# A decoder trunk on one core: where layer A's last block lies, when layer B's query weights are loaded, and which queue copies the window cache

## The chip, the cores and the metric

The kernel runs on one core of a Trainium2 chip. The metric is the device time of one execution in microseconds (us); lower is better.

## The reference

Four layers, A B C A, run over 1024 prompt tokens and 32 sample tokens (8 sequences of 4 new tokens, each with a cache of 4096 old ones), with width 1024. Every layer is `x = LayerNorm(ALPHA*x + mixer(x))`.

```python
def short_conv_mixer(x, buf, w_in, conv_w, w_out):            # layers 0 and 3 ("A")
    h, b_gate, c_gate, z = jnp.split(x @ w_in, 4, axis=-1)
    conv, new_buf = causal_dwconv(c_gate * h, buf, conv_w)
    return (jax.nn.silu(z) * b_gate * conv) @ w_out, new_buf
```

Layer 1 ("B") is an attention with three branches: keys and values compressed by blocks of 32 tokens, 16 selected blocks of 64 tokens, and a window of 512 tokens. The sample sequences read old keys and values through a page table, out of a paged cache (`cache_nsa_kv`) and a window cache (`cache_nsa_win`). Layer 2 ("C") is a gated linear recurrence. Besides the trunk's output the caches are returned. One of these outputs, `nsa_win_sample`, is the window cache moved on by four rows: 508 old rows of each of the 8 sequences, copied, and 4 new rows behind them.

## The kernel before, in words

**Precision and tiles.** Every matmul of float32 data is done as three: a tile is split into a high and a low part, and high x high, high x low and low x high are summed. Activations lie with features on the 128 partitions, as 8 tiles X[c] of 2 x 1056 columns. A product with a 1024 x 128 slice of weights ("a dense") is 24 matmuls for each third of the tokens (j = 0, 1, 2, with 352 columns each).

**Buffers.** There are 18 slots `big` (128 x 2112 words) and 3 slots `w` of the same size for split weights, a ring `ws` for raw weights and rows (4 slots in layer A, 1 of them set apart), a ring `c` of 8 tiles of 512 columns, and PSUM rings `mm` (5 banks) and `aux` (3 banks). A ring gives its slots in the order in which the program asks for them.

**The order of the work.** The functions don't issue instructions; they record steps (`Rec`, L241). `Rec.lay` (L378) then plays the steps through a simple model: each engine takes, of the steps that are ready, the one with the earliest due place in the program, and a transfer holds a common bus for its size divided by 360 bytes per ns. A transfer on SP's queue holds that queue for 100 ns. What comes out is the fixed order of PE, ACT, DVE and POOL. It covers three parts: layer 0 with the projections of layer B, the decode of layer B, and everything behind the attention. SP's own order is not fixed by hand (`manual_schedule` at the end of `Rec` names PE, ACT, DVE and POOL alone). The attention of the prompt has a planner of its own, which the change leaves as it is.

**Layer 0** (`layer_a`, L952): for each of 8 blocks c four denses (w = 0, 2, 3, 1: h, c_gate, z, b_gate), 96 steps of 24 matmuls in all. U[c], the block's result, is one `big` slot; it is written from the block's last dense on (w = 1). Beside it `compress` (L1296) goes through the paged cache: 64 gathers of 1 MB on POOL's queue, at most 3 ahead of the sums; two stores (`raw`) of 256 KB of each gathered tile; a multiply and sums on DVE or POOL. `share` (L610) lets the compress advance by RATE = 0.7 of a gather for each of the 96 steps.

**Behind it** `out_phase` (L685): the output product, 8 slices x 3 thirds, the sums of the norm, and the norm itself (`norm`), whose rows come back from DRAM (`dd`) through ring `c` and go out again to `xd` and `xs`. The weights of slice 7 lie in a `big` slot, the others in `w` slots. The first key weights of layer B (`first_b`) are fetched in its last third.

**The projections of layer B** (`b_project`, L1400): two halves, each over 9 tiles of 128 tokens in groups `g4` of four, four and one. Half 0 begins by loading four pieces of query weights WQ (512 KB each, split into `big` slots); each tile's 384 columns are copied by ACT out of PSUM into a tile `kv` of ring `c`, multiplied with the compression weights on POOL, and the group's keys are transposed and split by `put_k`, whose g = 1 branch stores the low parts to DRAM (`kl1`). The queries follow half 0 (`b_queries`).

**The decode** (`decode`, L1647): 36 units of keys and values, read from `raw`; the block selection for pairs 1 to 3 (`decode_select`, which reads the compressed keys from `kcd`) is put in at units SELT = 3, 9, 18.

**Layers 2 and 3** follow in one part, with `ws` of 5 slots. In the code of layer C, `gate_out` (L1189) holds the 8 copies of the window cache, on SP's queue; they touch no tile, and the mark `rk` that puts them behind `gate_out` is known to the planner alone.

Of the kernel before, what the change touches and what calls it, by code (L numbers as in the profile page):

```python
# [10 lines left out]
F32R = mybir.dt.float32r  # L11
# [7 lines left out]
P = 128  # L19
D = 1024  # L20
NCH = 8
# [9 lines left out]
LNW = 2112  # L31
# [209 lines left out]
class Rec:  # L241
# [136 lines left out]
    def lay(self):  # L378
# [45 lines left out]
        while True:  # L424
# [23 lines left out]
            if e == "SP":  # L448
                free[e] = s + 100
                bus = max(bus, s + 100) + o.size / 360  # L450
                o.end = bus + 2000
            else:
                free[e] = o.end = s + cost
                if o.size:
                    bus = max(bus, o.end) + o.size / 360
                    o.end = bus + 2000
# [42 lines left out]
class Trunk:  # L499
# [185 lines left out]
    def out_phase(self, pm, wsrc, U, X, ln, lp, res=None, done={}, spill=None, final=None, nxt=()):  # L685
# [13 lines left out]
        def take(c):  # L699
            for x in range(c, min(c + (3 if c != 4 else 4), NCH if c >= 4 else 7)):  # L700
                if x not in W and (ln, "out", x) not in self.pre:
                    src = wsrc[:, x * P:(x + 1) * P]
                    self.pre[(ln, "out", x)] = self.load_w(src, (ln, "out", x), slot=self.bp if x == NCH - 1 else None)
            W[c] = self.pre.pop((ln, "out", c))
# [247 lines left out]
    def layer_a(self, pm, a, X, lp, side=None, nxt=()):  # L952
# [3 lines left out]
        U = [None] * NCH  # L956
        SC = lp.tile([P, NCH, 36 if self.later else 18], F32, name="SC")
# [14 lines left out]
        for c in range(NCH):  # L972
# [6 lines left out]
            def step(w, j):  # L979
# [7 lines left out]
                if w == 0:  # L987
                    hs[j] = self.ct(TC)
                    nc.scalar.copy(hs[j], ps)
# [27 lines left out]
            U[c] = self.view2(self.big(F32R))  # L1017
# [66 lines left out]
    def layer_c(self, pm, X, lp):  # L1084
# [104 lines left out]
        def gate_out(c):  # L1189
# [13 lines left out]

            nc.sync.dma_start(win_s[c, 0:508, :], cache[c, 4:512, :], rk=[("z", c)])
# [20 lines left out]
        win_s = io["o_nsa_win_sample"][0].rearrange("b t c g d -> b t (c g d)")  # L1225
        cache = io["cache_nsa_win"][0].rearrange("b t c g d -> b t (c g d)")
# [173 lines left out]
    def b_project(self, pm, X, bs, ds):  # L1400
# [25 lines left out]
        def put_k(br, ps, g0, n):  # L1426


            for g in range(2):
# [13 lines left out]
        for half in range(2):  # L1443
            nw = 384 + 48 * half
            Wk = [self.get_w(("kv", half, k2), lambda: self.kv_weights(half, k2)) for k2 in range(4)]
            if half == 0:
                pc = self.aux(pm)[0:32, 0:256]
                side = iter(())
                WQ = {(0, k2): self.rows_w(k2, 0, 512, self.bp) for k2 in range(4)}
            else:  # L1450
                V = [kept()[:, 0:2048].rearrange("p (g t f) -> p g t f", g=2, t=8) for _ in range(2)]
            for g4 in ((0, 1, 2) if half == 0 else (2, 0, 1)):
                tts = range(4 * g4, min(4 * g4 + 4, 9))
                kn = []
                if half == 1 and g4 == 0:
                    side = self.decode_prepare(pm, q2, self.decode_gates(pm, GS, ds), KN, VN, ds)
                for tt in tts:
# [10 lines left out]
                    kv = self.ct(nw)  # L1468
# [765 lines left out]
RATE = 0.7  # L2234
# [20 lines left out]
SELT = (3, 9, 18)  # L2255
# [192 lines left out]
```

## Time and profile before

| | us |
|---|---|
| median of 3 runs (2403.86 to 2417.21) | 2408.07 |
| the profiled execution | 2407.38 |
| its span, first to last instruction | 2405.1 |
| PE busy in the span | 2303.5 |
| DVE, ACT, POOL busy | 1573.5, 1197.4, 963.3 |
| mean granted TensorE clock | 0.979 of full speed |

PE is the matrix engine, DVE the vector engine, ACT the scalar engine, POOL GpSimd, and SP the engine whose queue issues most transfers. A wait `A <- B` is time in which A sat idle until B's work released it. All planned steps have one source line (L310), since one helper records them; so the rows are told apart by their tiles (out<-in).

### The profile page before, as it was taken

Reading aid. Unit: us, or ns where it says so; the run is one execution under the profiler, and the core shown is the slowest. Engines: PE = TensorE matmul, PEld = TensorE weight load, DVE = VectorE, ACT = ScalarE, POOL = GpSimd, SP = SyncE. Lnnn points to the kernel's source line nnn. Section 1 sums busy time; section 2 is a strip of 40 time slices with the busy share of each in tenths; the row PEclk is TensorE's granted clock in tenths of the full one; section 3 lists DMA queues with packets and bytes.
Section 4 is the critical chain, followed back from the end, with each engine's and each line's share of the span. In section 5 each row is a group of like instructions: output and inputs, shape, how many; then the busy total and the mean of one; then the engine's idle time right before and its main releaser. Section 6 shows DMA issues by size and latency. Waiting matters only on the chain. (4 is left out here: it accounts for less than half of the span.)

```text
span 2405.1 us, 41388 instructions
## 1 busy us (share of the span) xinstructions
PE 2303.5 (96%) x14801; PEld 2233.7 (93%) x14801; DVE 1573.5 (65%) x3686; ACT 1197.4 (50%) x2753; POOL 963.3 (40%) x1070
## 2 busy tenths in 40 slices
PE   8999999897989989999999999999999999999996
PEld 8999998796888879999999998999999999999996
DVE  5776675565348876777777776798875753333336
ACT  3111121234438777888888883378873442222233
POOL 3454543313137855565555663233464320000230
PEclk9999999998999989999999999999999999999998
DMA  8999998438356751111111243341114321111012
GB/s 274 344 350 328 305 293 276 130 124 278 107 163 224 270 193 52 46 41 44 51 40 44 73 137 100 119 138 53 36 46 124 111 62 53 44 45 53 27 55 73
DMA packets 334642, 320.34 MB, mean 133 GB/s; under 512 B 19462, under 2 KB 301542, under 8 KB 324964
## 3 DMA queue, kind: packets, MB, share of 16 engines
q1 hardware_dynamic: 325220, 250.58, 33.9%
q0 software_dynamic: 9216, 67.11, 7.6%
q8 instruction: 117, 1.92, 0.3%
q14 instruction: 89, 0.73, 0.1%
HBM read 237.31 MB, written 84.48 MB: 134 GB/s over the span
## 5 line engine op out<-in xcount | busy, mean ns | idle before, releaser
L310 PE MATMUL mm<-x,w 128*128 128x352 f32 x5760 | 943.8, 325 | 19.0 <-DVE ws L310 10.5
L310 PEld LDWEIGHTS mm<-x,w 128*128 128x128 f32 x5760 | 933.4, 190 | 24.0 <-DVE ws L310 8.1
L310 PE MATMUL mm<-big,w 128*128 128x352 f32 x2208 | 379.5, 326 | 12.0 <-ACT big L310 9.6
L310 PEld LDWEIGHTS mm<-big,w 128*128 128x128 f32 x2208 | 358.0, 189 | 15.8 <-ACT big L310 9.9
L310 POOL TENSOR_TENSOR w<-ws,w 128x1024 fp32r<-128x1024 f32 (+1 forms) x43 | 105.9, 2462 | 419.2 <-ACT w L310 416.9
L1993 DVE TENSOR_TENSOR c<-T,c 128x512 fp32r<-128x512 f32 (+1 forms) x320 | 204.7, 648 | 49.5 <-ACT c L1989 44.8
L1989 ACT CAST c<-T 128x512 fp32r<-128x512 f32 (+1 forms) x320 | 174.5, 552 | 59.3 <-PE T L1985 38.3
L310 ACT CAST w<-ws 128x1024 fp32r<-128x1024 f32 (+2 forms) x116 | 120.3, 1038 | 161.8 <-PE mm L310 116.4
L641 PE MATMUL D<-x,w 128*128 128x352 f32 x1008 | 195.4, 330 | 2.2 <-DVE big L2120 2.2
L1895 PE MATMUL A<-big 128*128 128x320 f32 (+11 forms) x832 | 181.7, 334 | 3.4 <-DVE ast L1920 1.6
L2000 PE MATMUL O<-c,big 128*128 128x256 f32 x1056 | 180.4, 291 | 0.5 <-ACT c L1989 0.2
L310 POOL TENSOR_TENSOR big<-big,ws 128x1024 f32<-128x1024 f32 (+1 forms) x38 | 90.1, 2370 | 208.1 <-DMA big<-in_cache_nsa_kv,idx 101.7
L641 PEld LDWEIGHTS D<-x,w 128*128 128x128 f32 x1008 | 159.8, 188 | 5.7 <-DVE big L2120 3.5
L310 ACT CAST big<-aux 128x352 fp32r<-128x352 f32 (+3 forms) x116 | 45.4, 402 | 236.6 <-DVE aux L310 163.9
L310 DVE TENSOR_TENSOR w<-ws,w 128x1024 fp32r<-128x1024 f32 (+2 forms) x73 | 92.7, 1269 | 100.9 <-ACT w L310 100.3
L310 DVE TENSOR_TENSOR big<-big 128x256 f32<-128x256 f32 (+3 forms) x204 | 140.8, 711 | 24.1 <-POOL big L310 22.5
L2000 PEld LDWEIGHTS O<-c,big 128*128 128x128 f32 x1056 | 147.2, 189 | 2.6 <-DVE c L1993 0.7
L1953 POOL TENSOR_SCALAR pr<-pr,G,ast 128x32 f32<-128x32 f32 (+6 forms) x192 | 126.4, 672 | 47.0 <-DVE ast L1964 38.6
L1895 PEld LDWEIGHTS A<-big 128*128 128x128 f32 x832 | 134.4, 193 | 10.2 <-PE A L1895 2.2
L310 ACT ACTIVATE aux<-ws,PT 128x352 f32<-128x352 f32 (+2 forms) x72 | 42.5, 596 | 172.6 <-DVE ws L310 170.9
L1949 ACT ACTIVATE pr<-pr,ast 128x32 f32<-128x32 f32 (+6 forms) x192 | 118.4, 619 | 17.9 <-DVE ast L1920 16.8
L310 DVE SCALAR_TENSOR_TENSOR c<-c,mm 128x352 f32<-128x352 f32 x125 | 64.2, 516 | 88.6 <-ACT c L310 46.2
(286 smaller groups left out, 4031.1 us busy)
## 6 DMA issues: line engine op xcount, KB each, us to landing
ws<-in_a_w_in SPq DMA_DIRECT2D x64, 512.0 KB
raw<-big SPq DMA_DIRECT2D x128, 256.0 KB
big<-raw SPq DMA_DIRECT2D x128, 256.0 KB
c<-dd SPq DMA_DIRECT2D x48, 176.0 KB
xs<-x SPq DMA_DIRECT2D x24, 352.0 KB
x<-xs SPq DMA_DIRECT2D x8, 1056.0 KB
ws<-in_a_w_out SPq DMA_DIRECT2D x16, 512.0 KB
ws<-in_c_w_in SPq DMA_DIRECT2D x16, 512.0 KB
```

Of the source, the lines that this page charges most:

```text
L310: getattr(real, name)(*[f(x) for x in a], **{q: f(x) for q, x in k.items()})
L641: self.nc.tensor.matmul(ps, a, b, start=n == 0, stop=n == 23 and last)
L1895: nc.tensor.matmul(o, q[:, hl, i * P:(i + 1) * P], k, start=m == 0, stop=m == 1)
L1949: nc.scalar.activation(S[:, a:a + m], S[:, a:a + m], AF.Exp, bias=st[:, k:k + 1], scale=-1.0, accum_out=st[:, 3 + k:4 + k])
L1953: nc.gpsimd.tensor_scalar(S[:, a:a + m], S[:, a:a + m], G[:, i, 16 * k + h:16 * k + h + 1], st[:, 6 + k:7 + k], op0=ALU.mult, op1=ALU.mult)
L1989: nc.scalar.copy(x["H"][:, 0:n], x["tp"][:, 0:n])
L1993: nc.vector.tensor_sub(x["L"][:, 0:n], x["tp"][:, 0:n], x["H"][:, 0:n].bitcast(F32))
L2000: nc.tensor.matmul(O, v, M[:, y * P:(y + 2) * P], start=done[0] == 0, stop=done[0] == total - 1)
```

## The change

- The model of `Rec.lay` now counts 400 ns for an issue on SP's queue and 330 bytes per ns for the bus.
- Layer 0's U[7] takes a `w` slot instead of a `big` slot; in return the output weights of slices 6 and 7 lie in `big` slots (only 7 before). RATE goes from 0.7 to 0.75.
- The copies of the window cache leave layer C. They are now in the last layer (`layer_a` with no compress beside it), one for each block c, issued from ACT's queue, behind ACT's copy of the block's h for j = 2.
- In half 0 of layer B's projections the four pieces WQ are loaded in front of groups 1 and 2, two each, and not in front of group 0. The `kv` tiles of a group share one `big` slot (`four`) and leave ring `c`.
- `put_k` does g = 1 before g = 0. The selection's units SELT are 5, 10, 18.

```diff
--- before.py
+++ after.py
@@ -446,13 +446,13 @@
                     cost += 1283
                 table = f
             if e == "SP":
-                free[e] = s + 100
-                bus = max(bus, s + 100) + o.size / 360
+                free[e] = s + 400
+                bus = max(bus, s + 400) + o.size / 330
                 o.end = bus + 2000
             else:
                 free[e] = o.end = s + cost
                 if o.size:
-                    bus = max(bus, o.end) + o.size / 360
+                    bus = max(bus, o.end) + o.size / 330
                     o.end = bus + 2000
             order.append(o)
             o.start = s
@@ -700,7 +700,7 @@
             for x in range(c, min(c + (3 if c != 4 else 4), NCH if c >= 4 else 7)):
                 if x not in W and (ln, "out", x) not in self.pre:
                     src = wsrc[:, x * P:(x + 1) * P]
-                    self.pre[(ln, "out", x)] = self.load_w(src, (ln, "out", x), slot=self.bp if x == NCH - 1 else None)
+                    self.pre[(ln, "out", x)] = self.load_w(src, (ln, "out", x), slot=self.bp if x >= NCH - 1 - (ln == 0) else None)
             W[c] = self.pre.pop((ln, "out", c))
 
         def norm(j):
@@ -954,6 +954,7 @@
         stt = nc.vector.scalar_tensor_tensor
         win = io["a_w_in"][a]
         U = [None] * NCH
+        win_s, win_c = (io[x][0].rearrange("b t c g d -> b t (c g d)") for x in ("o_nsa_win_sample", "cache_nsa_win"))
         SC = lp.tile([P, NCH, 36 if self.later else 18], F32, name="SC")
         todo = [(w, c) for c in range(NCH) for w in (0, 2, 3, 1)]
         wkey = lambda x: ("a", a) + x
@@ -986,7 +987,10 @@
                 self.dense(ps, W[w], X, j)
                 if w == 0:
                     hs[j] = self.ct(TC)
-                    nc.scalar.copy(hs[j], ps)
+                    nc.scalar.copy(hs[j], ps, wk=[("h", a, c)] if j == 2 else [])
+                    if j == 2 and side is None:
+
+                        nc.scalar.dma_start(win_s[c, 0:508, :], win_c[c, 4:512, :], rk=[("h", a, c)])
                 elif w == 2:
                     nc.vector.tensor_mul(g[:, 2 + j * TC:2 + j * TC + np_], ps[:, 0:np_], hs[j][:, 0:np_])
                     if j == 2:
@@ -1014,7 +1018,8 @@
                             uv, uh, ul = (q.rearrange("p (b t) -> p b t", t=4) for q in (uv, uh, ul))
                         nc.vector.tensor_mul(v, uv, v)
                         self.split(uh, ul, v, "act", "dve")
-            U[c] = self.view2(self.big(F32R))
+
+            U[c] = self.view2(self.wp.tile([P, LNW], F32R, name="w", tag="w") if side is not None and c == NCH - 1 else self.big(F32R))
             if c == 0:
                 seq = [(w, j) for j in range(3) for w in (0, 2, 3)] + [(1, j) for j in range(3)]
             else:
@@ -1200,8 +1205,6 @@
                 stt(out=th, in0=th, scalar=1.0, in1=ps, op0=ALU.add, op1=ALU.mult)
                 stt(out=th, in0=th, scalar=0.5, in1=h2[:, i, sl], op0=ALU.mult, op1=ALU.mult, wk=[("z", c)])
                 self.split(u[:, 0, sl], u[:, 1, sl], th, "act", "pool")
-
-            nc.sync.dma_start(win_s[c, 0:508, :], cache[c, 4:512, :], rk=[("z", c)])
         UC, GT, WA, H = {}, {}, {}, {}
         todo = []
         for x in ORDER_C.split():
@@ -1222,8 +1225,6 @@
             for k in todo[i + 1:i + 2]:
                 fetch(k)
             return self.pre.pop(key)
-        win_s = io["o_nsa_win_sample"][0].rearrange("b t c g d -> b t (c g d)")
-        cache = io["cache_nsa_win"][0].rearrange("b t c g d -> b t (c g d)")
         for x in ORDER_C.split():
             c = int(x[1])
             if x[0] == "u":
@@ -1426,7 +1427,7 @@
         def put_k(br, ps, g0, n):
 
 
-            for g in range(2):
+            for g in (1, 0):
                 kd = K[br]
                 r0, r1 = slice(64 * g, 64 * g + 64), slice(64 - 64 * g, 128 - 64 * g)
                 sl = slice(g0, g0 + n)
@@ -1446,12 +1447,16 @@
             if half == 0:
                 pc = self.aux(pm)[0:32, 0:256]
                 side = iter(())
-                WQ = {(0, k2): self.rows_w(k2, 0, 512, self.bp) for k2 in range(4)}
+                WQ = {}
             else:
                 V = [kept()[:, 0:2048].rearrange("p (g t f) -> p g t f", g=2, t=8) for _ in range(2)]
             for g4 in ((0, 1, 2) if half == 0 else (2, 0, 1)):
                 tts = range(4 * g4, min(4 * g4 + 4, 9))
                 kn = []
+                four = self.big()
+                if half == 0 and g4:
+                    for k2 in (2 * g4 - 2, 2 * g4 - 1):
+                        WQ[0, k2] = self.rows_w(k2, 0, 512, self.bp)
                 if half == 1 and g4 == 0:
                     side = self.decode_prepare(pm, q2, self.decode_gates(pm, GS, ds), KN, VN, ds)
                 for tt in tts:
@@ -1465,7 +1470,7 @@
                             nc.tensor.matmul(ps, a, b, start=n == 0, stop=n == 23)
                             n += 1
                     next(side, None)
-                    kv = self.ct(nw)
+                    kv = four[:, len(kn) * nw:(len(kn) + 1) * nw]
                     if half == 0:
                         nc.scalar.copy(kv, ps)
                     else:
@@ -2231,7 +2236,7 @@
 FOFF = 7
 OUT0, OUTD, OUT1, OUTE = 119.07, 2.4, 114, 0.993
 OUTS = ((0, 0), (0, 1), (1, 0), (1, 1))
-RATE = 0.7
+RATE = 0.75
 GAHEAD = 3
 ORDER_C = "u101 u001 u12 u02 u2 g0 u5 z0 u3 g1 u4 g2 z1 z2 g3 u6 g4 u7 g5 z4 z3 g6 z6 z5 g7 z7"
 NLO = (((2, 5, 6, 7), (3, 4, 6), (0, 5)), ((6, 7), (0, 5, 7), (2, 7)), ((2, 4, 6, 7), (1, 2, 6), (0, 1, 2, 3, 6, 7)))
@@ -2252,7 +2257,7 @@
 TAILV = 39
 VLO = 0b10010010
 SEL0 = 1
-SELT = (3, 9, 18)
+SELT = (5, 10, 18)
 DSH = dict(sel=7.1, kin=-11.8, begin=-11.6, keys=2.2, score=-10.9, turn=30.4, pv=-26.1, vin=-88.9, first=-37.1, vals=-23.0,
        fin=17.8, fold=-41.1, weights=-59.0, exps=-96.3)
 DN = 3, 3, 3, 1
```

## Rows read from the trace of the kernel before

**Rows 1.** Page, part 1: busy us, share of span and count of each engine.
```profile
PE 2303.5 (96%) x14801; PEld 2233.7 (93%) x14801; DVE 1573.5 (65%) x3686; ACT 1197.4 (50%) x2753; POOL 963.3 (40%) x1070
```

**Rows 2.** Stretches: length, busy us (count) of PE, PEld, DVE, ACT, POOL; clock; DMA share; GB/s.
```profile
0.00:60.00 60.00, 53.19 (x329) 49.59 (x330) 31.27 (x67) 21.63 (x40) 19.22 (x18) 1.00 0.84 274
60.00:120.00 60.00, 60.00 (x375) 60.00 (x374) 45.76 (x73) 11.57 (x20) 27.62 (x16) 1.00 1.00 345
120.00:180.00 60.00, 60.00 (x376) 60.00 (x375) 46.77 (x72) 11.91 (x23) 33.60 (x20) 1.00 1.04 351
180.00:240.00 60.00, 55.80 (x332) 54.94 (x331) 41.09 (x67) 9.29 (x17) 25.44 (x15) 0.96 1.00 329
240.00:300.00 60.00, 57.80 (x351) 56.96 (x350) 39.00 (x68) 11.38 (x20) 33.88 (x17) 0.98 0.92 304
300.00:360.00 60.00, 56.35 (x332) 55.75 (x331) 42.99 (x73) 12.10 (x22) 28.33 (x16) 0.94 0.91 296
360.00:420.00 60.00, 54.02 (x315) 52.85 (x314) 36.25 (x66) 9.18 (x17) 21.52 (x13) 0.94 0.89 273
420.00:430.00 10.00, 1.80 (x12) 1.51 (x10) 4.38 (x6) 0.00 (x0) 5.21 (x3) 0.82 0.85 288
430.00:440.00 10.00, 6.55 (x23) 5.62 (x24) 7.67 (x17) 2.93 (x6) 0.50 (x1) 0.67 0.57 173
540.00:600.00 60.00, 45.16 (x209) 39.26 (x208) 37.05 (x67) 30.04 (x56) 23.45 (x22) 0.80 0.84 284
690.00:710.00 20.00, 13.20 (x74) 11.54 (x75) 10.38 (x27) 8.94 (x21) 4.27 (x6) 0.83 0.78 242
2040.00:2100.00 60.00, 60.00 (x376) 60.00 (x374) 21.58 (x40) 12.17 (x21) 0.00 (x0) 1.00 0.16 45
```

**Rows 3.** Tile out_nsa_win_sample: ns min/median/max of an issue, first and last start.
```profile
L310 SPq DMA_DIRECT2D out_nsa_win_sample<-in_cache_nsa_win x8: 529/1098/4707, 24.3 to 224.9; - x8
```

**Rows 4.** Timeline 385 to 470: start, length, instruction [idle before it <- releaser].
```profile
397.69 1.23 DVE L310 TENSOR_TENSOR big<-big,ws 128x1024 f32<-128x1024 f32 x1 [6.44 <-DMA big<-in_cache_nsa_kv,idx]
...
400.13 18.30 PE L310 MATMUL mm<-x,w 128*128 128x352 f32 x96 [3.11 <-DVE ws L310]
...
418.28 3.53 PE L310 MATMUL mm<-big,w 128*128 128x352 f32 x21
...
425.59 1.22 DVE L310 TENSOR_TENSOR big<-big,ws 128x1024 f32<-128x1024 f32 x1 [6.31 <-DMA big<-in_cache_nsa_kv,idx]
...
428.22 0.52 DVE L310 TENSOR_TENSOR aux<-c,aux 128x352 f32<-128x352 f32 x1
...
430.86 0.45 ACT L310 CAST big<-aux 128x352 fp32r<-128x352 f32 x1 [21.55 <-DMA raw<-big]
...
431.36 5.03 PE L310 MATMUL mm<-big,w 128*128 128x352 f32 x15 [9.56 <-ACT big L310]
...
438.91 4.30 PE L310 MATMUL mm<-big,w 128*128 128x352 f32 x24
```

**Rows 5.** Page, part 5: the split of a slice of weights, ACT's and POOL's part.
```profile
L310 POOL TENSOR_TENSOR w<-ws,w 128x1024 fp32r<-128x1024 f32 (+1 forms) x43 | 105.9, 2462 | 419.2 <-ACT w L310 416.9
...
L310 ACT CAST w<-ws 128x1024 fp32r<-128x1024 f32 (+2 forms) x116 | 120.3, 1038 | 161.8 <-PE mm L310 116.4
```

**Rows 6.** Timeline 571 to 610, the first groups of keys.
```profile
570.75 1.04 PE L310 MATMUL mm<-big,x 128*128 128x384 f32 x5
...
577.28 1.04 ACT L310 CAST big<-ws 128x1024 fp32r<-128x1024 f32 x1 [0.88 <-DMA ws<-in_b_w_in]
...
578.23 0.47 ACT L310 COPY c<-mm 128x384 f32<-128x384 f32 x1
...
578.36 1.22 DVE L310 TENSOR_TENSOR big<-ws,big 128x1024 fp32r<-128x1024 f32 x1 [0.23 <-ACT big L310]
...
578.76 2.29 PE L310 MATMUL mm<-w,x 128*128 128x384 f32 x6 [6.97 <-ACT c L310]
...
583.22 1.06 PE L310 MATMUL aux<-c,eb 128*32 128x256 f32 x2 [2.17 <-POOL c L310]
```

**Rows 7.** Timeline 684 to 718, the start of the decode.
```profile
693.92 0.69 DVE L310 TENSOR_TENSOR c<-aux,big 64x512 fp32r<-64x512 f32 x1 [0.86 <-issue]
694.64 0.49 SPq L310 DMA_DIRECT2D kl<-c  x1
...
697.60 0.32 SPq L310 DMA_DIRECT2D sel<-kcd  x1
...
698.11 1.28 DVE L310 TENSOR_TENSOR w<-mm,w 128x512 fp32r<-128x512 f32 x2
...
701.12 0.66 PE L310 MATMUL aux<-idf,sel 128*128 128x128 f32 x2 [6.80 <-DMA sel<-kcd]
```

## The prediction

> **What bounds the kernel now.** I read the page's shares first: PE is busy 2303.5 of 2405.1 us [rows 1], so whatever can be gained lies in PE's idle time and in the time for which its clock is low. Then I cut the span into stretches, to see where PE falls short [rows 2]. The measure is the count of matmuls: in 120 to 180 us PE does 376 in 60 us, 0.160 us each, without a gap, and in the last layer (2040 to 2100) 376 again. The four stretches from 180 to 420 hold 332, 351, 332 and 315, which is 1330 where 1504 would fit: 174 short, 27.8 us. In 420 to 440 there are 35 where 125 would fit: 90 short, 14.4 us. Layer 0 with its compress thus loses 42 us behind 180 us. In 540 to 600, where layer B's keys begin, PE idles 14.8 us and runs at a mean clock of 0.80 of full speed, so part of the stretch ran at the lower level, 1.2 GHz; a fifth of 45.2 busy us is another 9: 24 us. In 690 to 710, where the decode begins, it idles 6.8 us at 0.83 (some 2 us more): 9 us.
>
> Then I asked what limits the first stage. Its DMA share is 1.00 and 1.04 in 60 to 180, at 345 and 351 GB/s: the transfers are full while PE doesn't yet wait, and from 180 us on it waits. The timeline shows how [rows 4]: DVE takes its instructions in order, sits 6.44 us in front of a multiply whose gather hasn't landed (397.69), and PE waits 3.11 us for the product behind it. At the end of the block the same: DVE stands 6.31 us until 425.59, its part of U[7] is done at 428.74, the slot is still being read by a store (`raw`) until 430.86, and PE, which had used up its 21 matmuls that don't need U[7], waits 9.56 us and goes on at half speed: 15 matmuls take 5.03 us, where 24 take 4.30 later. So a late transfer ends last, in DVE's order.
>
> The row that decided most is that of the window cache's copies [rows 3]. They stand in layer C's code, but they touch no tile, SP's order is free, and they run at 24.3 to 224.9 us, in the very stage in which the transfers are full.
>
> **The change part by part.** The sum is made against the profiled execution, 2407.38 us (span 2405.1 and 2.3 around it); the median of three, 2408.07, is 0.7 above it.
>
> *The copies leave layer 0.* 8 x 508 KB is 4.16 MB; at 348 GB/s, the mean of the two full stretches, that is 12.0 us of transfer [rows 2, 3]. Issued by ACT, whose order is fixed by hand, they can't be pulled forward: they land in the last layer, where the transfers are 0.16 busy and ACT 12 of 60 us [rows 2]. There ACT pays 8 issues of 1.1 us, the median on SP, 4.7 us each at worst; ACT has 48 idle us of 60 and PE five banks, so I put it at 0, and at 9 us if that cover were gone. No row shows a transfer issued by ACT. For layer C nothing changes, since the copies never ran there.
> The Trainium skill ("DMA: Bandwidth & Descriptors", section "Issuing engines are not separate DMA queues") speaks against a gain from the new queue: transfers issued by several engines run on the same 16 DMA engines, and a second issuer saves only the issue time. By that rule alone the move would give 8 issues of 1.1 us on SP, which nobody waits for, so nothing; by the rows the gain is in the hour of the copies, not in their queue. No trace here shows a second issuer, so the rule can't be checked yet.
>
> *Bus of 330 and 400 ns an issue in the model, RATE 0.75, U[7] in a `w` slot.* Before, the model's bus gave 360 where the trace gives 348; over 180 us that is 6 us of drift, and from there on DVE's steps come ahead of their data. At 330 the model errs to the other side, so DVE stands less in front of a gather. RATE 0.75 ends the compress at step 85 of 96 and not at 91, so the last block's own DVE work is free of it. The wait for the slot of U[7] goes as far as the store causes it: 430.86 - 428.74 = 2.1 us. What is late next is the gathers themselves: up to 440 us some 135 MB move (rate times time of the stretches [rows 2]; 16 MB of them in the first 60 us), 131 MB without the copies, and at 348 GB/s from 60 us on that ends at about 390 us, near where PE alone would end (437 - 42 = 395). So the bounds of layer 0, the copies included, are 0 and -42 us. I take -20: the 12.0 of the copies, which are bytes, and 8 of the 30 others, since the gathers still fill the bus.
> The costs: two `w` slots are left for the output weights. Slice 5's weights get theirs when slice 3 is done, with 4.0 us of slice 4 to hide ACT's 1.04 and POOL's 2.46 [rows 5], so 0 to 3 us; U[7]'s slot comes free only with the block's last dense, and its split (0.45 and 0.53) hides behind the 3.53 us of matmuls that don't need it [rows 4]. I count both within the 20.
>
> *`kv` out of ring `c`, and WQ behind the first group.* Five tiles of keys are done by 571.8 us and fill the five banks; ACT's first copy comes at 578.23, behind a split of WQ (577.28), and PE waits 6.97 us, then 2.17 more on the product on POOL [rows 6]. The tile in ring `c` stands behind the norm's tiles in that ring's order; a `big` slot doesn't, so the copies can follow their matmuls and this wait goes. What is late next: the sixth tile needs the norm of the last third. Three of the four WQ splits stand on ACT (1.04 each) and on DVE or POOL ahead of it: 3 to 4 us earlier. So -4 for the wait, -2 for POOL's, -3 for the slow clock behind them: -9. The bounds: -24 (all that the stretch loses), and +6 if the last two pieces of WQ, asked for one tile ahead of their use, came late (1.05 MB at 348 GB/s is 3 us, a split 2.3).
>
> *SELT and `put_k`.* PE waits 6.80 us for the selection's keys, issued at 697.60 behind a `kl` store at 694.64 that waits for DVE [rows 7]. With the selection two units later and the store earlier the wait goes; but DVE's next keys are done only at 699.4 (698.11 + 1.28), so 1.5 of the 6.8 are certain and the rest open. I take -4, between +2 and -9.
>
> *The rest.* The model's new numbers reorder the output phases, layer C and the last layer, too. Those stretches wait little (none in 2040 to 2100), so there is little to gain: 0, within 8 to each side.
>
> Sum: -20 - 9 - 4 = -33; 2407.4 - 33 = 2374.
>
> **The rivals.** *All of layer 0's loss goes.* The copies were what tipped the stage over, and without them DVE never stands in front of a gather: -42 - 12 - 4, 2349 us. For it: the stage is full but not over-full in 60 to 180. Against it: at RATE 0.75 the compress asks for more per step than before.
>
> *Only the bytes count.* The reordering gives in one place what it takes in another, and the norm of the last third holds the sixth tile as long as before: -12, 2395 us.
>
> *The freed bus isn't used.* At most three gathers are in flight, and their next issue waits in POOL's order; then layer 0 keeps its time and only the kv copies' 4 us are won: 2403 us.
>
> *Slower: the compress in lock step.* RATE 0.75 places 64 gathers in front of step 85. If DVE stands in front of them as it does now, PE reaches step 85 when the last gather is summed; that is near 430 us now [rows 4], 418 without the copies; then 10.7 steps of 24 matmuls of 0.160 us, 41 us, are still to come, and the block ends at 459, where now the first output product is done at 436: some 23 us later, 2407 + 23 - 4 = 2426 us. It decides from the point at which the sums stand in DVE's order ahead of their data. Against it: the model's slower bus places the sums later than before, not earlier.
>
> **How the numbers follow.** The forecast, 2374 us, with 2362 to 2388 of its own, has a chance of 0.55; all of layer 0: 0.10; only the bytes: 0.17; the freed bus unused: 0.08; lock step: 0.10. The range of 2350 to 2412 leaves out the slower case and half of the best one. Half a per cent is 12 us (about what can be told from no change): the forecast nearly always, the best case and half of "only the bytes" are faster by more, which makes 0.72; the unused bus, the other half of the bytes and a little of the forecast are no change, 0.17; lock step is slower, 0.11.
>
> **What would show it.** The copies start behind 1950 us, on ACT's queue. The count in 180 to 420 rises from 1330 to over 1400, with DVE's waits for gathers shorter. PE has no wait of 9 us for U[7]. ACT's first copy of keys comes within a few us of its matmuls, and no wait of 7 us stands near 575; none of 6.8 near 700. The prediction is wrong if the copies still run early, if the sum of layer 0 moves by less than 8 us, or if the output phase loses to its two `w` slots what layer 0 wins.

## The result, and the profile after

The changed kernel takes 2380.38 us (median of 4 runs, 2374.68 to 2384.38); the kernel before, beside it, 2412.64 (4 runs, 2403.86 to 2417.50). The ratio is 0.987 [0.983, 0.991]. That is 32.3 us less by the medians (31.6 by the ratio), where 33 were forecast; the time itself is 6.4 us above the forecast of 2374 and inside its range. The profiled executions are 26.8 us apart (2407.38 and 2380.59; spans 2405.1 and 2378.4). The terms below are read from these two spans.

I cut both spans at the same five events: the first key matmul of layer B, the query matmul behind the last transpose of its keys (six query matmuls stand ahead of that in both), the first matmul of the decode, and the first and last of the prompt's attention.

| stretch, us | before | after | difference | forecast |
|---|---|---|---|---|
| start to first key matmul (layer 0 and its output phase) | 536.8 | 521.2 | -15.6 | -20 |
| first key to the queries | 72.4 | 61.5 | -10.8 | -9 |
| the queries, to decode | 80.5 | 80.5 | 0 | 0 |
| decode | 174.0 | 167.0 | -7.0 | -4 |
| attention (its planner was left alone) | 611.5 | 611.4 | -0.1 | 0 |
| behind it, to the end | 930.0 | 936.8 | +6.8 | 0, within 8 |

The sum is right and the four terms have the right sign or lie within their bounds. The reasons given for two of them, layer 0 and the decode, do not hold as given, as the experiments show. So the sum is right by luck in part.

The page of the kernel after, part 1, answers to [rows 1]: PE is busy 11.0 us less, and the span is 26.7 shorter, so some 16 us of idle time are gone.

```profile
PE 2292.5 (96%) x14801; PEld 2224.2 (94%) x14801; DVE 1589.8 (67%) x3686; ACT 1199.8 (50%) x2755; POOL 958.0 (40%) x1070
```

The stretches of layer 0 after, with the columns of [rows 2]:

```profile
60.00:120.00 60.00, 60.00 (x376) 60.00 (x375) 43.69 (x68) 9.57 (x17) 23.66 (x14) 1.00 0.90 296
120.00:180.00 60.00, 58.72 (x365) 58.44 (x365) 52.60 (x71) 13.74 (x25) 36.01 (x22) 1.00 0.98 329
180.00:240.00 60.00, 57.39 (x358) 57.10 (x357) 44.34 (x69) 9.96 (x19) 22.53 (x14) 1.00 0.97 318
240.00:300.00 60.00, 59.01 (x367) 58.60 (x365) 46.42 (x75) 13.43 (x24) 27.32 (x16) 1.00 0.95 301
300.00:360.00 60.00, 53.56 (x311) 52.81 (x310) 44.92 (x68) 9.29 (x17) 35.58 (x19) 0.94 0.87 286
360.00:420.00 60.00, 53.10 (x321) 52.15 (x320) 41.24 (x74) 10.42 (x19) 26.49 (x15) 0.95 0.98 305
```

The four stretches from 180 us hold 358, 367, 311 and 321 matmuls, 1357 against 1330: better, but not the 1400 and more that I had named as the sign. And the DMA columns contradict me: with 4.16 MB taken out, the stage from 60 to 180 moves 296 and 329 GB/s, where it moved 345 and 351. The room was not filled. The other half of that sign came true: in the first 400 us DVE waits less for gathers (us in total, times, longest; before, then after).

```profile
DVE big L310 <- DMA big<-in_cache_nsa_kv,idx: 18.9, 7, 6.4
```

```profile
DVE big L310 <- DMA big<-in_cache_nsa_kv,idx: 1.0, 2, 0.8
```

The tile `out_nsa_win_sample` after (ns min/median/max of an issue, first and last start), against [rows 3]: the copies are where I put them, in the last layer (which begins some 30 us earlier than I had reckoned), and ACT issues one in 517 ns.

```profile
L310 ACTq DMA_DIRECT2D out_nsa_win_sample<-in_cache_nsa_win x8: 517/517/647, 1919.1 to 2223.8; - x8
```

The timeline of PE after, around the first output product, against [rows 4] (start, length, instruction, idle before it and its releaser):

```profile
406.75 3.20 PE L310 MATMUL mm<-big,w 128*128 128x352 f32 x19
411.72 0.58 PE L310 MATMUL mm<-big,w 128*128 128x352 f32 x2 [1.76 <-DVE big L310]
415.25 0.66 PE L310 MATMUL mm<-w 128*128 128x352 f32 x1 [2.95 <-ACT w L310]
418.11 0.95 PE L310 MATMUL mm<-w 128*128 128x352 f32 x2 [2.20 <-DVE w L310]
```

The first output product comes at 406.75 instead of 418.28. The wait of 9.56 us for U[7] is gone; in its place stand three, 6.9 us together: one for a part of another block (`big`, by DVE), two for the high and the low part of U[7] in its `w` slot (by ACT and DVE).

PE's waits after, from the first key matmul to the queries (us in total, times, longest): the 7.0 us for ACT's copy of keys [rows 6] are gone, and what holds PE now is the norm's `x`.

```profile
PE mm L310 <- ACT x L310: 3.5, 3, 2.1
PE mm L310 <- POOL x L310: 0.9, 2, 0.7
```

The start of the decode after, against [rows 7]: `sel` is still issued 2.5 us behind the `kl` store, but PE comes for it later and waits 2.60 us instead of 6.80.

```profile
664.71 0.49 SPq L310 DMA_DIRECT2D kl<-c  x1
...
667.21 0.36 SPq L310 DMA_DIRECT2D sel<-kcd  x1
...
673.65 0.41 PE L310 MATMUL aux<-idf,sel 128*128 128x128 f32 x2 [2.60 <-DMA sel<-kcd]
```

### The profile page after: what moved, and what is told of

The parts are those of the page before. It is cut to its first block, busy times and chain, and to the rows that moved or that the text cites. A ratio compares the mean times of both kernels' runs of the same rounds, so it can differ in the third digit from the quotient of the medians.

```text
span 2378.4 us, 41368 instructions
## 1 busy us (share of the span) xinstructions
PE 2292.5 (96%) x14801; PEld 2224.2 (94%) x14801; DVE 1589.8 (67%) x3686; ACT 1199.8 (50%) x2755; POOL 958.0 (40%) x1070
## 3 DMA queue, kind: packets, MB, share of 16 engines
q10 hardware_dynamic: 256, 4.16, 0.5%
## 5 line engine op out<-in xcount | busy, mean ns | idle before, releaser
L310 PE MATMUL mm<-big,w 128*128 128x352 f32 x2082 | 361.5, 328 | 6.9 <-DVE c L310 3.5
L310 PEld LDWEIGHTS mm<-big,w 128*128 128x128 f32 x2082 | 341.1, 191 | 10.3 <-DVE c L310 4.1
L310 DVE TENSOR_TENSOR big<-big 128x256 f32<-128x256 f32 (+3 forms) x204 | 173.2, 869 | 20.8 <-POOL big L310 18.8
L310 POOL TENSOR_TENSOR big<-big 128x512 fp32r<-128x512 f32 (+2 forms) x74 | 86.4, 1186 | 106.3 <-DVE big L310 83.2
L1954 ACT ACTIVATE pr<-pr,ast 128x32 f32<-128x32 f32 (+6 forms) x192 | 118.4, 619 | 18.9 <-DVE ast L1925 18.1
L310 DVE SCALAR_TENSOR_TENSOR aux<-ws,PT,aux 128x352 f32<-128x352 f32 (+1 forms) x168 | 97.2, 590 | 22.5 <-ACT aux L310 20.2
```

The source lines that it names most:

```text
L310: getattr(real, name)(*[f(x) for x in a], **{q: f(x) for q, x in k.items()})
L1954: nc.scalar.activation(S[:, a:a + m], S[:, a:a + m], AF.Exp, bias=st[:, k:k + 1], scale=-1.0, accum_out=st[:, 3 + k:4 + k])
```

## The experiments

Theory at the start: layer 0 wins by the bytes of the copies first, and by the model's numbers second. Rival: bytes don't count there, since at most three gathers are in flight. All times are medians, with the ratio to the kernel before run beside them on the same chip (2408.09, 2408.75 and 2411.26 us in the three groups of runs). Each profile shows one execution only. Two kernels whose orders agree on all five engines up to 531 us (the changed one and `kv` back in ring `c`, below) start the first output product 7.9 us apart and the first key matmul 6.3 us apart in their profiles, so a difference of that size between two single profiles shows nothing by itself.

### The copies

**The copies alone, on the kernel before.** Layer C's line goes, layer A gets the two lines.

```
+                    if j == 2 and side is None:
+                        nc.scalar.dma_start(win_s[c, 0:508, :], win_c[c, 4:512, :], rk=[("h", a, c)])
...
-            nc.sync.dma_start(win_s[c, 0:508, :], cache[c, 4:512, :], rk=[("z", c)])
```

> The kernel before with one part of the change alone: the copies issued by ACT in the last layer. Theory 'bytes': the first key matmul (536.7 us before) comes some 12 us earlier and the whole is 10 to 14 us below before (2412 median): about 2400. Rival 'order': nothing above 4 us is won, since DVE's steps stay in front of their gathers in the old order.

Measured: 2409.88 us (10 runs), 1.001 [0.9995, 1.0025]. Nothing is won. Its two full stretches:

```profile
60.00:120.00 60.00, 60.00 (x375) 60.00 (x375) 43.98 (x76) 11.71 (x20) 27.59 (x16) 1.00 0.96 321
120.00:180.00 60.00, 59.76 (x372) 59.47 (x371) 44.32 (x70) 12.01 (x23) 35.47 (x20) 1.00 0.96 313
```

The rate falls by 24 and 38 GB/s, some 3.7 MB over the two stretches, which is nearly what was taken out. The other transfers did not move up. SP's `raw` stores and weight loads came out in another order here, too, since that order isn't written out; what the run shows is that both together bring nothing.

**The changed kernel with the copies back in layer C's code** (the same lines the other way round).

> The changed kernel, but with the 8 copies of the window cache back in layer C's code on SP's queue; all else as changed. Theory 'bytes': the copies run again in the first 250 us, take 12 us of full transfer time out of layer 0, and all of it is lost: the first key matmul (521.2 us in the changed kernel's profile) comes 8 to 14 us later, the whole 8 to 14 us above the changed kernel (2380). Rival 'order': the gain of layer 0 came from the planner's numbers and U[7]; the copies fill gaps of the transfers: first key matmul within 3 us, the whole within 4 us of the changed kernel.

Measured: 2373.13 us (4 runs), 0.9855 [0.9828, 0.9882]. A loss of 8 to 14 us was the bytes' forecast; the median is 7 us *below* the changed kernel's (3 us by the ratios, whose intervals overlap), so there is no loss to be seen. The copies ran at 25.4 to 196.4 us again, the first output product came at 400.17 instead of 406.75, and the stage moved about as much as in the kernel before, in 180 to 240 us more:

```profile
60.00:120.00 60.00, 60.00 (x375) 60.00 (x374) 48.22 (x74) 11.94 (x22) 27.57 (x18) 1.00 1.04 348
120.00:180.00 60.00, 60.00 (x376) 60.00 (x375) 52.66 (x71) 11.85 (x22) 34.58 (x20) 1.00 1.00 336
180.00:240.00 60.00, 60.00 (x375) 60.00 (x375) 44.18 (x82) 13.00 (x23) 21.10 (x14) 1.00 1.03 346
```

With those bytes in it, PE does 375 or 376 in every stretch from 60 to 240 us. But again SP's stores and loads had come out in another order, so this run does not separate bytes from order either.

**The copies on ACT's queue, but in layer 0.**

```
-                    if j == 2 and side is None:
+                    if j == 2 and side is not None:
```

> The changed kernel, but ACT issues the copies in layer 0, one for each block, instead of in the last layer. Theory 'the hour, not the queue': as the copies on SP's queue in layer 0, 8 to 14 us above the changed kernel. Rival 'the queue': a second issuer takes the copies out of SP's way (its issues took up to 4.7 us), so that layer 0 loses less than 4 us.

Measured: 2384.48 us (4 runs), 0.9898 [0.9869, 0.9927], with the copies at 47.9 to 389.4 us: 4 us above the changed kernel, with overlapping ranges, and 11 us above the run just shown, which has the same copies in layer 0 on SP's queue. Here too SP's order was another.

### SP's order held

**SP's order written out like the others'.** One word; PE, ACT, DVE and POOL keep exactly the instructions and order of the changed kernel.

```
-        with self.tc.manual_schedule(engines={E.PE, E.Activation, E.DVE, E.Pool}):
+        with self.tc.manual_schedule(engines={E.PE, E.Activation, E.DVE, E.Pool, E.SP}):
```

> The changed kernel with SP's order fixed by the planner too, so that the copies can be moved without anything else moving. It is the base for the next run; alone it says whether SP's free order costs anything: theory 'the free order is a matter of luck' 2372 to 2390; rival 'the free order is good' 2395 or more, since the planner's order knows the transfers less well.

Measured: 2362.08 us (4 runs, 2359.45 to 2366.64), 0.9805 [0.9779, 0.9832]: 18 us below the changed kernel by the medians and 15 by the ratios (their intervals just touch, the ranges of the runs do not), by SP's order alone. That is below what either theory had. In the profile, the fastest of the four, the first output product comes 16.1 us earlier, at 390.64, and PE has no gap from 60 to 360 us:

```profile
180.00:240.00 60.00, 60.00 (x376) 60.00 (x375) 48.93 (x81) 12.60 (x22) 23.76 (x14) 1.00 1.01 330
240.00:300.00 60.00, 60.00 (x375) 60.00 (x374) 52.14 (x76) 11.96 (x20) 35.59 (x20) 1.00 0.96 318
300.00:360.00 60.00, 60.00 (x376) 60.00 (x375) 42.63 (x73) 10.67 (x20) 30.02 (x18) 1.00 0.97 316
```

The waits from 0 to 400 us show through what. In the changed kernel SP stands 125.1 us in front of `raw` stores whose gather hasn't landed, and behind them wait the loads of the compression weights that DVE and POOL need:

```profile
SPq L310 <- DMA big<-in_cache_nsa_kv,idx: 125.1, 27, 13.9
DVE big L310 <- DMA ws<-in_b_w_cmp: 37.5, 6, 10.0
POOL big L310 <- DMA ws<-in_b_w_cmp: 56.6, 4, 20.0
```

With SP's order fixed each of these is smaller. SP does not stand less in all: it now waits 45.3 us for splits by POOL, where it waited 2.8. Less of it stands in front of gathers:

```profile
SPq L310 <- DMA big<-in_cache_nsa_kv,idx: 70.2, 22, 9.7
SPq L310 <- POOL w L310: 45.3, 8, 7.3
DVE big L310 <- DMA ws<-in_b_w_cmp: 18.9, 6, 7.5
POOL big L310 <- DMA ws<-in_b_w_cmp: 45.5, 5, 12.0
```

**The same, and the copies by ACT in layer 0.** SP's order is now identical to the run above, so only the copies' place differs there (the edit of the copies in layer 0, on top of SP's).

> As the run with SP's order fixed, but ACT issues the copies in layer 0, one for each block. PE's, DVE's, POOL's and SP's order in layer 0 are the same in both, so the difference is the price of 4.16 MB in layer 0. Theory 'bytes': 8 to 14 us slower than with the copies in the last layer, the first output product as much later. Rival 'the gathers' chain sets the pace' (at most three in flight, each waits for the sum of the third before it): the copies fill gaps, less than 4 us.

Measured: 2364.83 us (4 runs, 2359.83 to 2369.51), 0.9805 [0.9774, 0.9836]. The medians are 2.7 us apart, the ratios the same, and the ranges overlap. The two profiles, of this kernel's second slowest run and of the other's fastest, are 9.2 us apart: the first output product is 5.6 us later and the first key matmul 9.0 (SP's order fixed, then with the copies in layer 0):

```profile
390.64 3.53 PE L310 MATMUL mm<-big,w 128*128 128x352 f32 x21
...
502.28 6.57 PE L310 MATMUL mm<-w,x 128*128 128x384 f32 x36
```

```profile
396.25 3.20 PE L310 MATMUL mm<-big,w 128*128 128x352 f32 x19
...
511.27 6.56 PE L310 MATMUL mm<-w,x 128*128 128x384 f32 x36
```

So the 4.16 MB cost layer 0 some 3 us by the medians, and anything from nothing to 9 can't be excluded. Nothing here shows the 12.

The Trainium skill ("DMA: Bandwidth & Descriptors", section "Issuing engines are not separate DMA queues") says that a second issuer saves only the time of the issue. No run here shows it either way, since none moves the copies from SP's queue to ACT's in the same stage with SP's order held: the two runs that differ so are 11 us apart (2373.13 and 2384.48), in another order of SP's. What the runs show is the size of the issues: 8 x 517 ns is 4.1 us on ACT's queue, and on SP's they took 641 to 911 ns each with the copies back. The prediction's words that no trace showed a second issuer overlook POOL's queue, which issues the gathers; none showed a plain copy from ACT's.

### How many gathers are in flight

**Four ahead and not three**, with the copies back in layer C's code.

```
-GAHEAD = 3
+GAHEAD = 4
```

> The kernel with the copies back on SP's queue in layer C's code (2373 us) and four gathers ahead instead of three. Theory 'the chain sets the pace': the last gather (415.8 us there) is issued 10 us or more earlier and the first output product (400.2) starts 5 to 15 us earlier: 2358 to 2368. Rival 'bytes': the transfers are full, the gathers land later in proportion and nothing is won: within 4 us of 2373, or slower, as DVE stands in front of them longer.

Measured: 2365.81 us (5 runs), 0.9822 [0.9796, 0.9848], against 0.9855 [0.9828, 0.9882] with three: 7 to 8 us, though the intervals still overlap. In the profile, which is of the fastest of the five runs, the last gather is issued at 406.08 instead of 415.78, the first output product comes 8.5 us earlier, and the stage carries more than what I had taken for its limit:

```profile
60.00:120.00 60.00, 60.00 (x376) 60.00 (x375) 49.15 (x82) 12.58 (x22) 31.57 (x17) 1.00 1.01 357
120.00:180.00 60.00, 60.00 (x375) 60.00 (x375) 48.36 (x73) 12.84 (x23) 37.56 (x20) 1.00 1.03 348
180.00:240.00 60.00, 60.00 (x375) 60.00 (x374) 48.34 (x77) 12.47 (x22) 24.48 (x15) 1.00 1.05 356
```

That 348 GB/s was a mean and not a ceiling can also be read in finer slices. The rate in 120 to 240 us, by slices of 3 us, runs from 124 to 420 GB/s in the changed kernel, and from 175 to 420 in the kernel before, where I could have read it before the prediction (changed kernel, then before):

```profile
GB/s 310 372 416 325 339 330 280 363 333 308 292 124 287 246 332 342 414 338 412 420 396 347 385 329 189 290 176 150 377 298 318 404 365 346 394 389 341 334 193 334
```

```profile
GB/s 382 343 419 413 361 349 380 208 281 360 371 309 343 320 343 378 420 339 327 363 387 335 302 232 295 382 418 346 276 285 335 311 382 343 175 339 400 411 312 311
```

### The model's numbers

**The changed kernel with the old model**, 100 ns an issue and 360 bytes per ns.

```
-                free[e] = s + 400
-                bus = max(bus, s + 400) + o.size / 330
+                free[e] = s + 100
+                bus = max(bus, s + 100) + o.size / 360
...
-                    bus = max(bus, o.end) + o.size / 330
+                    bus = max(bus, o.end) + o.size / 360
```

> The changed kernel with the planner's old numbers (100 ns an issue on SP, bus of 360 bytes per ns). Theory: the new numbers give layer 0 some 5 to 10 us and take some 7 us in layer C (the changed kernel loses 6.8 us behind the attention against before). So the first key matmul comes 5 to 10 us later than 521.2 and the stretch behind the attention is 5 to 8 us shorter (937 instead of 944 us from the attention's last O product to the end): within 4 us of the changed kernel in all. Rival: the numbers do nothing for layer 0, and the loss in layer C comes from the other edits: first key matmul within 3 us of 521, layer C as slow as now.

Measured: 2398.7 us (10 runs), 0.9959 [0.9944, 0.9974]. The whole was expected within 4 us of the changed kernel; it is 18 above. So the numbers, with the order of SP that came of them, bring 18 us, and all other edits together the 9 that this kernel is below the one before, about what the ring of `kv` and WQ's place are worth below (5.6 and 3.1). By the spans (19.0 in all): 14.4 up to the first key matmul, 2.3 in the keys, 9.4 in the decode; 6.0 are lost behind the attention and 1.0 in it. The size in layer 0 can't be told from SP's order, which is not held here either; the sign can. Over the fourteen profiles of this document, the first key matmul comes at 535.6 to 539.3 us in the three kernels with the old numbers there, and at 501.1 to 527.6 in the eleven with the new ones. The decode of this kernel, then of the changed kernel, then of the kernel before (columns of [rows 2]):

```profile
679.80:856.20 176.40, 160.30 (x1077) 142.40 (x1075) 140.24 (x340) 126.02 (x238) 119.14 (x109) 0.96 0.75 256
```

```profile
663.20:830.20 167.00, 154.87 (x1076) 137.20 (x1075) 135.64 (x340) 125.97 (x238) 118.29 (x108) 1.00 0.75 261
```

```profile
689.60:863.60 174.00, 159.41 (x1078) 142.26 (x1076) 135.90 (x340) 126.19 (x238) 119.29 (x110) 0.96 0.72 244
```

With SELT and `put_k` as changed but the old model, PE no longer waits for `sel` (nothing but 1.2 us idle is left in front of it), and the decode is still 2.4 us longer than before, at a granted clock of 0.96: PE waits for DVE instead, 4.3 us for `w` and 5.6 for `pt`, which were 0 and 0.6 in the kernel before. Only with the new numbers is the clock 1.00, and PE's own time 4.5 us less than before. The three kernels with the old numbers take 172.9 to 176.4 us for the decode, the eleven with the new ones 165.9 to 169.5.

**The old numbers only for the part behind the attention**, with the copies back in layer C's code.

```
+        self.SPN, self.BUS = 400, 330
...
         k.later = 1
+        k.rec.SPN, k.rec.BUS = 100, 360
```

> The kernel with the copies back on SP's queue in layer C's code (2373 us), and the planner's old numbers for the part behind the attention alone. Theory: the new numbers cost that part some 5 us (from the attention's last product to the final phase 821 to 823 us with them, 817 to 818 with the old ones): 817 us there and 2366 to 2370 in all, the fastest so far. Rival: the spread of that stretch is chance or comes from the other edits: 821 us or more, 2373.

Measured: 2368.6 us (4 runs), 0.9828 [0.9804, 0.9853], 4.5 below the run with the copies back, as expected; the stretch from the last matmul of the attention to the last layer's final sums went from 821.6 to 818.3 (before 816.6, changed kernel 823.4). So the numbers that help layer 0 cost some 3 to 6 us behind the attention: there PE waits 3.5 us for DVE's `c` tiles with them and 1.1 without. Over the fourteen profiles that stretch is 816.6 to 818.4 us with the old numbers (four kernels) and 818.8 to 823.4 with the new ones (ten).

### The other parts, one at a time

**RATE back at 0.7** (`RATE = 0.75` to `RATE = 0.7`).

> The changed kernel with RATE 0.7 instead of 0.75. Theory 'the model's slower bus carries layer 0': the order is then set by the modelled arrival of the gathers and not by RATE, so the first output product (406.8 us in the changed kernel's profile) starts within 4 us and the whole is within 5 us of 2380. Rival 'the sooner the gathers are asked for, the better': 6 steps of the block are given back to waits for gathers, the first output product starts 8 us or more later, the whole 2388 or more. Rival 'lock step': with fewer gathers in front of each step layer 0 gets faster by 5 us or more.

Measured: 2377.7 us (4 runs), 0.988 [0.9862, 0.9898]. The rate makes no difference that can be measured.

**U[7] back in a `big` slot**, and only slice 7's weights in a `big` slot (the lines are cut short).

```
-            U[c] = self.view2(self.wp.tile(...) if side is not None and c == NCH - 1 else self.big(F32R))
+            U[c] = self.view2(self.big(F32R))
...
-    slot=self.bp if x >= NCH - 1 - (ln == 0) else None
+    slot=self.bp if x == NCH - 1 else None
```

> The changed kernel with U[7] in a big slot and slice 6's weights in a w slot again. Theory: in the changed kernel PE pays 6.9 us in three waits at the first output product (for ACT and DVE, whose work on U[7] had to wait for the slot of the block's last weights), against 9.6 us for the store before; so undoing it changes the first key matmul (521.2) by less than 4 us, to either side. Rival 'the slot was the point': without it U[7] stands behind the last gathers' stores again, 8 us or more later.

Measured: 2379.78 us (4 runs), 0.988 [0.9863, 0.9898]. The old wait is back, whole (the first row begins with the view):

```profile
419.73 2.10 PE L310 MATMUL mm<-big,w 128*128 128x352 f32 x12
431.73 4.74 PE L310 MATMUL mm<-big,w 128*128 128x352 f32 x14 [9.89 <-ACT big L310]
```

Yet the first key matmul comes only 2.5 us later and the time is the same. The edit trades one wait of 9.9 us for three of 6.9, and what it wins is lost again behind.

**WQ loaded in front again** (the two loads move back before group 0).

```
-                WQ = {}
+                WQ = {(0, k2): self.rows_w(k2, 0, 512, self.bp) for k2 in range(4)}
...
-                if half == 0 and g4:
-                    for k2 in (2 * g4 - 2, 2 * g4 - 1):
-                        WQ[0, k2] = self.rows_w(k2, 0, 512, self.bp)
```

> The changed kernel with the four pieces of query weights loaded in front of the first group of keys again; the kv tiles stay in their big slot. Theory 'both': the splits (1.04 on ACT, 1.2 to 2.6 on DVE or POOL, three of them early) cost the stretch from the first key matmul to the first query product (61.5 us in the changed kernel, 72.4 before) 3 to 5 us. Rival 'the ring was all': within 1.5 us of 61.5. Rival 'the load was all': 70 us or more.

Measured: 2382.09 us (4 runs), 0.9893 [0.9877, 0.991]. The stretch of keys is 64.7 us instead of 61.5, and PE waits for an ACT split. So WQ's place is worth some 3.2 of the 10.8 us.

```profile
PE mm L310 <- ACT big L310: 6.0, 2, 5.3
```

**`kv` back in ring `c`** (`kv = self.ct(nw)`, and `four` goes).

> The changed kernel with the kv tiles in ring c again; the query weights stay behind the first group. Theory: the tiles stand behind the norm's in the ring's order, so the copies come late and PE waits with five full banks: the stretch from the first key matmul to the first query product is 66 to 70 us (61.5 in the changed kernel). Rival 'the load was all': within 1.5 us of 61.5.

Measured: 2385.92 us (4 runs), 0.9904 [0.9887, 0.992]: 5.5 us slower. The wait of the kernel before is back:

```profile
PE mm L310 <- ACT c L310: 7.5, 1, 7.5
```

The stretch of keys can't be cut here as in the other kernels, since PE's order is another one: 24 query matmuls, and not six, stand ahead of the last transpose of keys, and the first of them comes 61.7 us behind the first key matmul with products of the keys still to do. So I take keys and queries together, from the first key matmul to the decode: the same 720 matmuls in the kernel before, the changed kernel, this one, and the one with WQ in front (columns of [rows 2]).

```profile
536.70:689.60 152.90, 137.99 (x720) 121.74 (x719) 70.42 (x187) 64.48 (x153) 41.22 (x46) 0.92 0.54 175
```

```profile
521.20:663.20 142.00, 134.40 (x720) 118.04 (x719) 70.03 (x187) 64.42 (x153) 42.52 (x46) 0.98 0.54 178
```

```profile
527.50:675.10 147.60, 135.45 (x720) 119.51 (x719) 69.07 (x187) 64.54 (x153) 42.06 (x46) 0.95 0.56 181
```

```profile
521.20:666.30 145.10, 133.89 (x720) 117.56 (x719) 71.60 (x187) 63.51 (x153) 41.36 (x46) 0.98 0.54 176
```

So the ring is worth 5.6 us, and WQ's place 3.1, of 10.9. All the other kernels with both edits in take 140.9 to 144.2 us here, so the 5.6 are clear of their spread. Measured so, the theory holds: its 66 to 70 us were 4.5 to 8.5 more than 61.5. The profile as a whole is 8.2 us longer than the changed kernel's; 6.3 of these stand in front of the first key matmul (and 3.7 are won back behind the projections), where the orders of all five engines agree (changed kernel, then this one):

```profile
521.17 6.57 PE L310 MATMUL mm<-w,x 128*128 128x384 f32 x36
```

```profile
527.51 6.56 PE L310 MATMUL mm<-w,x 128*128 128x384 f32 x36
```

## Why the prediction was right in size and wrong in a step

**The copies, 12.0 us: wrong.** The step that failed is "8 x 508 KB is 4.16 MB; at 348 GB/s, the mean of the two full stretches, that is 12.0 us of transfer", taken as a gain. Alone the move wins nothing (ratio 1.001); undone it loses nothing; with SP's order held it is worth about 3 us, at the most some 9. I had read a DMA share of 1.00 as a limit. What the runs point to as the pace is a chain: three gathers in flight, the next behind a sum, the sum behind a compression weight, that weight behind a `raw` store in SP's order. That SP's order counts is shown (15 to 18 us by it alone); that it acts through these loads is read from the waits; the depth of three is likely (7 to 8 us, with SP's order not held). The rival "the freed bus isn't used" had the gathers' part of this mechanism, at 0.08, but tied it to a time of 2403, since it gave the model's numbers nothing.

**The model, 8 us: right in kind, too small, and in too few places.** DVE does stand less in front of late data: in the first 400 us it waits 68.8 us for transfers before, 62.7 in the changed kernel with the old numbers, 39.5 with the new. But little of that is gathers, which I had named: those waits are 18.9, 3.8 and 1.0, so most of them had gone without the numbers; the rest is weights and `raw` stores. The numbers are worth 14.4 us up to the first keys in the one pair of profiles, with SP's order as it came. That makes up for the copies: 15.6 measured, 20 forecast. I had argued it only for layer 0. In the decode it brings 9.4, and behind the attention it costs 6.0.

**U[7] and RATE, within the 20: nothing.** My sign, no 9 us wait for U[7], came true and was worth nothing that can be measured. I had put slice 5's weights at 0 to 3 us; no wait of PE there names that slot. The waits that came are for the parts of the last blocks, 6.9 us: U[7]'s split did not hide behind the matmuls that don't need it.

**The keys, -9: right, -10.8, and for the reasons given.** I had put 6 for PE's waits and 3 for the slow clock behind them. Over keys and queries together PE is idle 7.3 us less (the waits for ACT's and POOL's `c`, 7.0 and 2.5, are gone) and busy 3.6 us less for the same matmuls, at a granted clock of 0.98 instead of 0.92. Undone one at a time, the ring is worth 5.6 us and WQ's place 3.1. What I had named as next, the norm's `x`, is what PE waits for now.

**SELT and `put_k`, -4: right sign, -7.0, another cause.** PE's wait fell by 4.2 us. With the old model, though, the same edits leave the decode no shorter than before. SELT and `put_k` were not undone one by one, so their own share stays open.

**The rest, 0 within 8: +6.8,** by the model's numbers. ACT's eight issues cost little there, as forecast, at 517 ns each and not 1.1 us: with the copies alone moved that part is 818.4 us against 816.6.

**The sum.** That it came out has to do with luck: the 12 us of the copies did not come, the model's numbers gave more than their 8, and the unforeseen 3 us of the decode went against 6.8 behind the attention. SP's order was luck as well. Five kernels that differ in nothing but SP's order and the place of the copies, the changed one among them, lie from 2362 to 2384 us.

**What stays open.** Whether the 7 us between the run with the copies back and the changed kernel are SP's order or chance: it was not run with only that difference. What the model's numbers are worth in layer 0 with SP's order held. Fixed order, four gathers ahead and the old numbers behind the attention were not tried together.

## What to carry to other kernels

A DMA share of 1.00 was not yet a limit here: take bytes away in thought and ask who would use the room, and if the next transfer waits for a sum or a store, look at that chain first. Before an edit is credited with a gain, hold every queue's order, the DMA-issuing queue's too; here any moved transfer reshuffled it, and its order was worth up to 18 us. A planner's transfer model that errs to the slow side kept DVE from standing in front of late data, but its numbers belong to a stage: what helped the full one cost some microseconds in the empty one. And before a stretch is compared between two kernels, look whether the same work lies in it: an event that marks its end can move to another place in the order.

## What the runs showed of the hardware that was not expected

The same DRAM-to-DRAM copy of 508 KB holds ACT's queue for 517 ns in the last layer and in the full stage alike (at most 647), where SP's queue took 529 to 4707 in the full stage [rows 3], and 641 to 911 with the copies back there in the changed kernel. With the copies alone moved to ACT's queue, and to the last layer with it, SP was spared these issues, and the time stayed the same (1.001).

The decode has the same 1077 matmuls, within one, in all three kernels; at a granted clock of 1.00 instead of 0.96 they kept PE busy 154.9 us instead of 159.4. Of the 7.0 us won there, 4.5 are PE's busy time and 2.5 are idle time.
